# Seven products instead of eight for the last eight pairs of output tiles of the fifth stage, in a decoder step on one core

## The chip, the cores and the metric

The kernel runs on one core of one Trainium2 chip. The metric is the device time of one execution in microseconds; the figures shown are medians of several executions. TensorE does the matrix products, VectorE (DVE) and ScalarE (ACT) work elementwise, GpSimd (POOL) fills buffers and issues some of the DMAs, SyncE (SP) issues the others.

## The reference

1024 prompt tokens and 8 decode tokens, 2048 wide, in fp32, pass through two layers: a pooling layer A, then shared keys and values, then an attention layer B. Cut to what matters here:

```python
# layer A
z = x @ w_in_a                      # 2048 -> 4096: branch u and gate
d = einsum(pool(u) - u, w_grp_a) * scale_a
h = layer_norm(ALPHA * x + (d * silu(gate)) @ w_out_a)
# shared keys and values, 4 heads of 64
kv = h @ w_kv                       # k gets a partial rotary
# layer B: 32 query heads, window of 128, one learned sink per head
z = h @ w_in_b                      # 2048 -> 4096: q and gate
q = rope_partial(z[:, :2048])
o = softmax(q k^T / 8, masked, with sink) @ v
y = layer_norm(ALPHA * h + (o * silu(gate)) @ w_out_b)
```

## The kernel before

**Precision.** A product of fp32 matrices is made on TensorE as three matmuls. Each operand is split into a high part (a cast on ScalarE, L423 for weights, L686 for inputs) and a low part (a subtract on VectorE, L438 and L695). TensorE then forms high x high, high x low and low x high.

**Stages.** Tokens come in two chunks: chunk 0 has 512, chunk 1 has 520 (with the decode tokens). The stages stand in `PHASES`: `ai` (input product of A, with pooling), `ao` (output product of A), `bi` (keys, values, queries and gates, with the attention inside), `bo` (output product of B), each for chunk 0 and then chunk 1. `ai` of chunk 0 is listed as two parts, so `bi` of chunk 0, called the fifth stage here, is the sixth entry of `PHASES`; the sixth stage is `bi` of chunk 1.

**Two ways to multiply.** A stage in `PLAIN` uses `unit`: one output tile of 128 rows is 48 matmuls of 512 columns (L614 to L616). All others use `seven`: the two output tiles of a pair, the even and odd halves of the inner dimension and the two halves of the tokens form a 2 x 2 x 2 block product, which is done with seven products instead of eight (Strassen's way, in Winograd's form). One product is 24 matmuls of 256 or 260 columns (L586 to L588), so a pair takes 168 matmuls of half width where two units take 96 of full width. `ORDER7` and `ORDERL` are orders of the seven products. In exchange `seven` needs sums of weight blocks and sums of input blocks. Before the change `bi` of chunk 0 is plain.

**Weight sums.** A plain stage loads the four blocks of a pair, and `plain_pair` forms the four sums afterwards (L254) and stores them to DRAM; the later chunk loads them in `next_pair`. `first_pair` is for a first chunk that already uses seven products: it forms the sums (L307) ahead of their use and stores them too. For the output weights of B, `sum_gen("wob")` is a side generator: 32 parts, each two loads of 256 KB, three adds (L397 to L399) and a store; half of the parts run in the fifth stage and half in the sixth.

**Input sums.** The sums of the inputs (T1 to T4) are made by `t_ops` (four adds, L741 to L744, and a store), called by `t_gen` (a generator that loads the activations again), by `ln_gen` (the layer norm) or, for the attention's output o, by `gate`. They lie in `Td`.

**Order.** All weight blocks form one `stream`. `begin` runs ahead of TensorE by a fixed number of blocks: load, cast, subtract (7, 4, 3 in stages with seven products, 5, 4, 3 in plain ones). `end` counts steps, runs events due at that step and, every so many steps (`every`), one step of a side generator, if enough of the 53 buffers are free (`room`). Inputs of the next stage are prepared by `x_begin`, `x_tick` and `x_get`: X blocks are loaded (L676), cast and subtracted some steps ahead; at the latest they are made when first asked for. The program order of TensorE, VectorE and ScalarE is the order of the source (`in_order`). Loads are issued on SP's queue, stores of sums on POOL's.

**Attention.** `attend` strings out one tile's work over steps: score (L1456), selection and largest value (L1473 to L1485), exponentials, totals, norm, transposes (`turn`, L1509), copies (L1518, L1519), values (L1533) and the gate (L1542, then a store of o). `q_done` applies the rotary (L1321), which needs a copy of the query with partitions swapped: four DMAs on SP's queue (L1313), then the sum (L1428).

Where a stage of chunk 1 follows one of chunk 0 that also used seven products, three dummy matmuls (L574, `fresh`) stand at its start.

Of the kernel before, what the change touches and what calls it, by code (L numbers as in the profile page):

```python
# [50 lines left out]
    ("ai", 0, (0, 1)), ("ai", 0, (1, 4)), ("ai", 1, (0, 4)), ("ao", 0, None), ("ao", 1, None), ("bi", 0, None),  # L51
    ("bi", 1, None), ("bo", 0, None), ("bo", 1, None),
# [107 lines left out]
class Kern:  # L160
# [132 lines left out]
    def first_pair(self, name, q):  # L293

        a11, a12, a21, a22 = self.quads(name, q)
        ws = self.ws[name][q]
        s = {}

        def load(k, src):
            return self.load1(s, k, src)  # L300

        def add(out, x, y, i):
            def go():
                assert self.prepped >= self.made - 2
                if out not in s:
                    s[out] = self.mem.full()
                self.nc.vector.tensor_add(s[out].a[:, :1024], s[x].a[:, :1024], s[y].a[:, :1024])  # L307
# [26 lines left out]
    def build_stream(self):  # L334
        io = self.io
        w = []
        for kind, c, part in PHASES:
# [4 lines left out]
            if kind == "ai":  # L342
                for g in range(*part):
                    for q in (2 * g, 2 * g + 1, 8 + 2 * g, 9 + 2 * g):
                        w += pr("wia", q)
                    for h in range(2):
                        w.append(self.lone(io["wg"][g][:, h * 1024 : (h + 1) * 1024]))
            elif kind == "bi":
                w += self.next_pairs("wkv", range(2), locked) if seven else pr("wkv", 0) + pr("wkv", 1)
                for p in range(8):  # L350
                    if seven:
                        w += pr("wib", p) + pr("wib", 8 + p)
                    else:
# [14 lines left out]
    def sum_gen(self, name):  # L368
# [15 lines left out]
        for n, (q, cs) in enumerate(parts):  # L384
            one = self.ph == "bi1"
            while one and n not in held and len(self.mem.whole()) < 6 and self.hurry is not name:
                yield
            load(n)
            if not one:
                load(n + 1)  # L390
            yield
            if one:
                yield
            s = held.pop(n)
            t = s.v(4, W)
            add = self.nc.vector.tensor_add
            add(t[:, 0:2, :], t[:, 0:2, :], t[:, 1:3, :])  # L397
            add(t[:, 2, :], t[:, 2, :], t[:, 0, :])
            add(t[:, 3, :], t[:, 3, :], t[:, 2, :])  # L399
            self.nc.gpsimd.dma_start(self.ws[name][q][:, :, cs], t)  # L400
            s.free(True)
            if n % 4 == 3:
                self.summed[name] = q + 1
            yield
# [392 lines left out]
    def ln_gen(self, c, pre, acc, gc, bc, out, td):  # L797
# [29 lines left out]
        else:  # L827
            sq, sqs = self.mem.full(), {}
            for p in range(10):
# [4 lines left out]
                if 1 <= p <= 8:  # L834
                    sqs[p - 1] = sq if p == 1 else self.mem.full()
                    nc.scalar.activation(flat(sqs[p - 1]), flat(pre[p - 1]), AF.Square)
                if p > 2:
# [24 lines left out]
        for p in range(10):  # L862
# [6 lines left out]
            if 1 <= p <= 8:  # L869
                affine(p - 1)  # L870
                if td is None:
                    pre[p - 1].free(True)
            if p >= 2 and td is not None:
# [568 lines left out]
    def attend(self, c, t, at, s1, s2, late=False):  # L1442
# [96 lines left out]
        def gate():  # L1539
            a = self.ao[c, t] = self.mem.half()  # L1540
# [5 lines left out]
            if c == 1 or ("o", c) not in self.Td:  # L1546
                self.ao.pop((c, t)).free(True)
            elif t % 2:
                e = self.ao.pop((c, t - 1))
                self.t_ops(e.a[:, :TP], a.a[:, :TP], self.Td["o", c], t // 2, T // 2)  # L1550
                e.free(True)
                self.ao.pop((c, t)).free(True)
# [139 lines left out]
    def phase_bi(self, c, nxt):  # L1692
        nc = self.nc
        T = CHUNKS[c][1]
        self.kv_open(c)
        if not self.strassen:
# [12 lines left out]
            for t in range(16):  # L1709
# [14 lines left out]
                self.last = t == 15  # L1724
# [3 lines left out]
        pairs = []  # L1728
        for done in (self.k_done, self.v_done):
            box, z0, z1 = self.two(T)  # L1730
            pairs.append((z0, z1, lambda done=done, box=box: done(c, box["s"])))
        self.both(c, *pairs)
        for p in range(8):
# [6 lines left out]
            box, z0, z1 = self.two(T)  # L1740
            if p == 7:
                self.x_begin(nxt)
                self.ahead = 6, 3, 2
            self.pair(c, z0, z1, lambda t0=t0, box=box: self.q_done(c, t0, box["s"], 2, 3))
            self.last = p == 7

            def g_done(t0=t0, box=None, p=p):
                self.gate_done(c, t0, box["s"], 2)
# [3 lines left out]
            box, z0, z1 = self.two(T)  # L1752
            self.pair(c, z0, z1, lambda g=g_done, box=box: g(box=box))
# [30 lines left out]
    def run(self):  # L1784
# [3 lines left out]
        self.sg, self.qs, self.ao = {}, {}, {}  # L1788
# [10 lines left out]
        for n, (kind, c, part) in enumerate(PHASES):  # L1799
# [6 lines left out]
            if n == 0 or (kind, c) == ("bi", 0):  # L1806
# [24 lines left out]
            elif (kind, c) == ("ao", 1):  # L1831
                gen = self.ln_gen(0, *acc[0], C_GA, C_BA, self.act["h", 0], self.Td.get(("h", 0)))
                self.at(3, lambda gen=gen: add(("h", 0, True), gen))
                self.every = 2
            elif (kind, c) == ("bi", 0):
                add(("h", 1, False), self.ln_gen(1, *acc[1], C_GA, C_BA, self.act["h", 1], self.Td.get(("h", 1))))
                self.summed["wob"] = 0
                add("wob", self.sum_gen("wob"))
                self.every = 2
            elif (kind, c) == ("bi", 1):  # L1840
                self.every, self.room = 1, 99
                self.at(14, lambda: setattr(self, "room", 0))
# [11 lines left out]
            elif kind == "bi":  # L1854
                self.phase_bi(c, nxt)
# [148 lines left out]
```

## Time and profile before

| | |
|---|---|
| median of 3 executions | 2384.65 us (2382.46 to 2386.11) |
| the profiled execution | 2384.47 us, its span 2382.7 us |
| mean granted TensorE clock | 0.996 |
| TensorE busy | 2341.7 us, 98% |
| VectorE busy | 1875.5 us, 79% |
| ScalarE busy | 1305.6 us, 55% |
| DMA | 653.25 MB, mean 274 GB/s |

In a row of a group stand the line, the engine, the operation, output <- input, the shapes, the count, then the busy time and the mean of one in ns, then the idle time of the engine just before and what ended it. In a row of a timeline stand the start, the duration, and in brackets the idle time before and its releaser. Matmuls are pipelined, so the duration of one (281 ns) is longer than the distance to the next. In the profile the stages begin at these times of the span: `ai` of chunk 0 at 8.0 (its seven-product part at 111.4), `ai` of chunk 1 at 384.2, `ao` at 755.5 and 916, the fifth stage at 1081.7, the sixth at about 1554, `bo` at 2025 and 2183.4.

### The profile page before, as it was taken

What the parts mean: (1) busy time and instruction counts of PE and PEld (TensorE: products, weight loads), DVE (VectorE), ACT (ScalarE), POOL (GpSimd) and SP (SyncE); (2) the same over time, 40 slices, a digit from 0 to 9 for tenths busy, and PEclk for the clock granted to TensorE, in tenths of its full rate; (3) what the DMA queues carried; (4) which work ended last, traced back from release to release, by engine and by line L of the source; (5) the groups of instructions that cost most, each with busy time, mean ns of one, the idle gap of its engine ahead of it and who ended that gap; (6) DMA issues with size and microseconds to landing.
All of it is one profiled execution on the core that took longest, in us unless ns stands there. A gap on an engine that the chain in (4) does not pass through costs nothing. (4 is left out here: it accounts for less than half of the span.)

```text
span 2382.7 us, 45063 instructions
## 1 busy us (share of the span) xinstructions
PE 2341.7 (98%) x17823; PEld 2198.5 (92%) x17823; DVE 1875.5 (79%) x2327; ACT 1305.6 (55%) x2363; POOL 192.3 (8%) x361
## 2 busy tenths in 40 slices
PE   8999999999999999999999999999999999999996
PEld 6899999999999999998778888899999999999996
DVE  8797999776788768868787777778777667789877
ACT  4454446454446447653564444475666667546655
POOL 0111110000000000000011111101000000000000
PEclk9999999999999999999999999999999999999998
DMA  8767779998889988988587777589786558799884
GB/s 292 243 220 277 257 255 379 310 307 299 299 297 352 313 276 313 353 294 285 186 322 261 263 269 247 202 285 303 254 244 208 173 177 296 226 337 364 303 281 141
DMA packets 250563, 653.25 MB, mean 274 GB/s; under 512 B 25456, under 2 KB 109168, under 8 KB 250352
## 3 DMA queue, kind: packets, MB, share of 16 engines
q1 hardware_dynamic: 206032, 489.50, 61.9%
q0 software_dynamic: 44320, 160.88, 17.5%
q8 instruction: 139, 2.28, 0.4%
q14 instruction: 72, 0.59, 0.1%
HBM read 459.41 MB, written 181.36 MB: 269 GB/s over the span
## 5 line engine op out<-in xcount | busy, mean ns | idle before, releaser
L586 PE MATMUL pD<-m,m 128*128 128x260 f32 (+1 forms) x4304 | 1220.8, 284 | 5.4 <-DVE m L547 3.4
L588 PE MATMUL pD<-m,m 128*128 128x260 f32 (+1 forms) x4304 | 1213.0, 282 | 2.7 <-DVE m L438 2.7
L587 PE MATMUL pD<-m,m 128*128 128x260 f32 (+1 forms) x4304 | 1213.8, 282 | 0.0
L438 DVE TENSOR_TENSOR m<-m,m 128x1024 fp32r<-128x1024 f32 x650 | 785.5, 1219 | 102.4 <-ACT m L423 69.9
L586 PEld LDWEIGHTS pD<-m,m 128*128 128x128 f32 x4304 | 810.8, 188 | 14.2 <-issue 7.6
L588 PEld LDWEIGHTS pD<-m,m 128*128 128x128 f32 x4304 | 811.3, 188 | 3.7 <-DVE m L438 3.5
L587 PEld LDWEIGHTS pD<-m,m 128*128 128x128 f32 x4304 | 810.8, 188 | 1.6 <-issue 1.4
L423 ACT CAST m<-m 128x1024 fp32r<-128x1024 f32 x650 | 676.2, 1048 | 242.8 <-DVE m L307 55.5
L614 PE MATMUL pD<-m,m 128*128 128x512 f32 x704 | 281.6, 400 | 8.0 <-ACT m L686 8.0
L615 PE MATMUL pD<-m,m 128*128 128x512 f32 x704 | 278.4, 395 | 0.8 <-DVE m L695 0.8
L616 PE MATMUL pD<-m,m 128*128 128x512 f32 x704 | 278.1, 395 | 0.0
L614 PEld LDWEIGHTS pD<-m,m 128*128 128x128 f32 x704 | 133.1, 189 | 42.7 <-ACT m L686 8.0
L615 PEld LDWEIGHTS pD<-m,m 128*128 128x128 f32 x704 | 133.2, 189 | 31.4 <-DVE m L695 1.9
L616 PEld LDWEIGHTS pD<-m,m 128*128 128x128 f32 x704 | 133.0, 189 | 30.6
L695 DVE TENSOR_TENSOR m<-m,m 128x1024 fp32r<-128x1024 f32 (+1 forms) x114 | 139.4, 1226 | 10.0 <-ACT m L686 4.3
L686 ACT CAST m<-m 128x1024 fp32r<-128x1024 f32 (+1 forms) x114 | 119.6, 1053 | 19.2 <-PE pD L616 6.2
L559 ACT COPY m<-pD 128x260 f32<-128x260 f32 (+1 forms) x75 | 28.0, 373 | 184.8 <-PE pD L588 184.4
L254 DVE TENSOR_TENSOR m<-m,m 128x1024 f32<-128x1024 f32 x88 | 107.5, 1222 | 1.9
L1492 ACT ACTIVATE m<-m,sm 128x128 f32<-128x128 f32 x256 | 99.3, 390 | 0.0
L547 DVE TENSOR_TENSOR m<-pD,m 128x260 f32<-128x260 f32 (+1 forms) x78 | 33.1, 424 | 80.7 <-PE pD L588 80.6
L954 PE MATMUL pD<-m,m 128*128 128x260 f32 (+1 forms) x528 | 91.3, 323 | 0.0
L552 DVE TENSOR_TENSOR m<-pD,m 128x260 f32<-128x260 f32 (+1 forms) x76 | 32.2, 424 | 71.1 <-PE pD L588 71.1
(197 smaller groups left out, 2136.2 us busy)
## 6 DMA issues: line engine op xcount, KB each, us to landing
m<-in_wia SPq DMA_DIRECT2D x112, 512.0 KB, 7.1
m<-in_wib SPq DMA_DIRECT2D x112, 512.0 KB, 4.9
swia<-m POOLq DMA_DIRECT2D x64, 512.0 KB, 4.8
m<-swia SPq DMA_DIRECT2D x64, 512.0 KB, 7.0
m<-swoa SPq DMA_DIRECT2D x64, 512.0 KB, 6.9
swib<-m POOLq DMA_DIRECT2D x64, 512.0 KB, 5.0
m<-swib SPq DMA_DIRECT2D x64, 512.0 KB, 5.1
m<-swob SPq DMA_DIRECT2D x64, 512.0 KB, 6.5
```

The lines of the kernel that those rows point to most:

```text
L254: self.nc.vector.tensor_add(s[out].a[:, :1024], s[a].a[:, :1024], s[b].a[:, :1024])
L423: self.nc.scalar.copy(hi.r[:, :1024], self.stream[self.cast].src().a[:, :1024])
L438: self.nc.vector.tensor_sub(lo.r[:, :1024], s.src().a[:, :1024], hi.a[:, :1024])
L586: nc.tensor.matmul(ps[:, :TH], wh[:, s], h, start=new and k == 0, stop=False, skip_group_check=on)
L587: nc.tensor.matmul(ps[:, :TH], wh[:, s], l, start=False, stop=False, skip_group_check=on)
L588: nc.tensor.matmul(ps[:, :TH], wl[:, s], h, start=False, stop=k == 7, skip_group_check=on)
L614: nc.tensor.matmul(ps[:], wh[:, s], h, start=par == 0 and k == 0, stop=False)
L615: nc.tensor.matmul(ps[:], wh[:, s], l, start=False, stop=False)
L616: nc.tensor.matmul(ps[:], wl[:, s], h, start=False, stop=par == 1 and k == 7)
L686: self.nc.scalar.copy(h.r[:, :n], s.a[:, :n])
L695: self.nc.vector.tensor_sub(l.r[:, :n], s.a[:, :n], h.a[:, :n])
L1492: nc.scalar.activation(x["s3"][:, i, :], x["s3"][:, i, :], AF.Exp, bias=nm[:, i : i + 1], scale=0.125, accum_out=rs[:, i : i + 1],)
```

## The change

The fifth stage is cut in two entries of `PHASES`. Keys, values and the first four pairs of query tiles and of gate tiles stay plain. The last four pairs of query tiles and four pairs of gate tiles use `seven`. For that the X blocks of the second half are loaded, cast and subtracted anew in the form that `seven` reads, and the sums of h of chunk 0 are made by a `t_gen` in the first half (load, four adds, store, for eight parts).

The weights of these eight pairs now go through `first_pair`: seven blocks per pair are cast and subtracted instead of four, and the four sums come ahead of their use. `first_pair` itself changes: the block a22 is no longer kept from product 2 to product 6 but is added in place and loaded a second time. This holds for the first stage too.

The sums of the output weights (`sum_gen`) run wholly in the sixth stage, with other rules for when a part is loaded and when it is added. The input sums over o of chunk 0 are no longer made in `gate` but by a `t_gen` in the sixth stage. `ln_gen` pauses more often, and the side generators of the first half step every 1.2 steps instead of every 2. The sixth stage now follows one with seven products, so it gets the dummy matmuls of `fresh`. Counted over the whole program the change adds 579 matmuls (768 of 512 columns go, 1344 of 256 columns and three dummies come), 70 instructions on VectorE, 58 on ScalarE, 34 DMA issues on SP and 8 on POOL.

```diff
 PHASES = (
-    ("ai", 0, (0, 1)), ("ai", 0, (1, 4)), ("ai", 1, (0, 4)), ("ao", 0, None), ("ao", 1, None), ("bi", 0, None),
-    ("bi", 1, None), ("bo", 0, None), ("bo", 1, None),
+    ("ai", 0, (0, 1)), ("ai", 0, (1, 4)), ("ai", 1, (0, 4)), ("ao", 0, None), ("ao", 1, None), ("bi", 0, (0, 4)),
+    ("bi", 0, (4, 8)), ("bi", 1, (0, 8)), ("bo", 0, None), ("bo", 1, None),
 )
...
             0: ent("a", [load("a", a11)], [], []),
-            2: ent("e", [load("b", a21), load("c", a22)], [add("e", "b", "c", 1)], []),
+            2: ent("e", [load("b", a21), load("e", a22)], [add("e", "b", "e", 1)], []),
...
-            6: ent("c", [], [], free("c")),
+            6: ent("c", [load("c", a22)], [], free("c")),
...
-        for n, (q, cs) in enumerate(parts):
-            one = self.ph == "bi1"
-            while one and n not in held and len(self.mem.whole()) < 6 and self.hurry is not name:
-                yield
-            load(n)
-            if not one:
-                load(n + 1)
-            yield
-            if one:
-                yield
-            s = held.pop(n)
+        def add(n):
+            q, cs = parts[n]
+            s = held[n]
...
+        if self.ph == "bi1":
+
+            since, n = {}, 0
+            while n < len(parts):
+                hurry = self.hurry is name
+                if n in held and (hurry or self.i - since[n] >= 3):
+                    yield from add(n)
+                    n += 1
+                m = n + len(held)
+                if m < len(parts) and (len(held) < 2 and len(self.mem.whole()) > 5 + len(held) or hurry and not held):
+                    load(m)
+                    since[m] = self.i
+                yield
+            return
...
                     nc.scalar.activation(flat(sqs[p - 1]), flat(pre[p - 1]), AF.Square)
+                yield
...
+            if td is not None:
+                yield
             if p >= 2 and td is not None:
...
         def gate():
-            a = self.ao[c, t] = self.mem.half()
+            a = self.mem.half()
...
-            elif t % 2:
-                e = self.ao.pop((c, t - 1))
-                self.t_ops(e.a[:, :TP], a.a[:, :TP], self.Td["o", c], t // 2, T // 2)
...
-            for t in range(16):
+            for t in range(2 * ps[0], 2 * ps[-1] + 2):
...
-                self.attend(c, t, 8, {13: 13, 15: 11}.get(t, 14), 2, t > 13)
+                self.attend(c, t, 8, 14 if t <= 2 * ps[-1] else 9, 2)
                 self.unit(q_done)
-                if t == 12:
+                if t == 2 * ps[-1] + 0:
                     self.x_begin(nxt)
...
-            if n == 0 or (kind, c) == ("bi", 0):
+            if n == 0 or (kind, c) == ("bi", 0) and self.wide:
...
-                gen = self.ln_gen(0, *acc[0], C_GA, C_BA, self.act["h", 0], self.Td.get(("h", 0)))
+                gen = self.ln_gen(0, *acc[0], C_GA, C_BA, self.act["h", 0], None)
...
-            elif (kind, c) == ("bi", 0):
+            elif (kind, c) == ("bi", 0) and not self.strassen:
                 add(("h", 1, False), self.ln_gen(1, *acc[1], C_GA, C_BA, self.act["h", 1], self.Td.get(("h", 1))))
+                add(("h", 0, False), self.t_gen(("h", 0)))
+                self.every = 1.2
+            elif (kind, c) == ("bi", 1):
                 self.summed["wob"] = 0
-                add("wob", self.sum_gen("wob"))
-                self.every = 2
-            elif (kind, c) == ("bi", 1):
-                self.every, self.room = 1, 99
-                self.at(14, lambda: setattr(self, "room", 0))
+                self.at(14, lambda: add("wob", self.sum_gen("wob")))
+                self.at(14, lambda: add(("o", 0, False), self.t_gen(("o", 0))))
+                self.every, self.room = 1, 0
```

More of the change, by code (lines that the diff above doesn't have):

```diff
@@ L348, in build_stream @@
             elif kind == "bi":
[L349 to L351 removed]
+                if part[0] == 0:
+                    w += self.next_pairs("wkv", range(2), locked) if seven else pr("wkv", 0) + pr("wkv", 1)
+                if seven:
+                    for p in range(*part):
                         w += pr("wib", p) + pr("wib", 8 + p)
[L353 removed]
+                else:
+                    for p in range(*part):
                         q, g = pr("wib", p), pr("wib", 8 + p)
@@ L403, in sum_gen @@
                 self.summed[name] = q + 1
+        if self.ph == "bi1":
[11 more added lines that the diff above has]
+            return
+        for n in range(len(parts)):
+            load(n)
+            load(n + 1)
+            yield
+            yield from add(n)
             yield
@@ L1727, in phase_bi, with queries @@
             return
[L1728 to L1733, printed above, removed]
+        if ps[0] == 0:
+            pairs = []
+            for done in (self.k_done, self.v_done):
+                box, z0, z1 = self.two(T)
+                pairs.append((z0, z1, lambda done=done, box=box: done(c, box["s"])))
+            self.both(c, *pairs)
+        def queries(p):
             t0 = 2 * p
@@ L1854, in run @@
             elif kind == "bi":
-                self.phase_bi(c, nxt)
+                self.phase_bi(c, range(*part), nxt)
             else:
```

36 lines of the change are left out of this document (21 added, 15 removed).

## The prediction

> **What bounds the kernel now.** I read the page's engine totals first, then its costliest groups, then the busy time of each engine by stage, then TensorE's timeline.
>
> ```profile
> span 2382.7 us, 45063 instructions
> PE 2341.7 (98%) x17823; PEld 2198.5 (92%) x17823; DVE 1875.5 (79%) x2327; ACT 1305.6 (55%) x2363; POOL 192.3 (8%) x361
> ```
> ```profile
> 111.40:125.00 13.60, 13.60 (x117) 13.55 (x116) 13.57 (x13) 8.47 (x12) 1.30 (x4) 1.00 0.79 276
> 111.40:384.20 272.80, 271.56 (x2162) 265.02 (x2161) 244.19 (x291) 137.26 (x196) 32.80 (x71) 1.00 0.75 263
> 384.20:755.50 371.30, 369.42 (x3077) 368.82 (x3076) 289.71 (x435) 180.02 (x284) 30.36 (x48) 1.00 0.91 314
> 1430.00:1554.00 124.00, 124.00 (x684) 100.41 (x681) 90.10 (x115) 63.76 (x163) 17.73 (x34) 1.00 0.67 225
> 1554.00:2025.00 471.00, 469.97 (x4186) 454.56 (x4186) 345.36 (x439) 313.34 (x718) 22.15 (x36) 1.00 0.75 242
> 1722.00:1822.00 100.00, 100.00 (x912) 96.76 (x911) 72.87 (x95) 65.20 (x161) 5.80 (x9) 1.00 0.75 235
> ```
>
> TensorE is busy for 98% of the span. In the last part of the fifth stage (1430 to 1554) and in the middle of the sixth (1722 to 1822) it never stands: there, time is TensorE's work and nothing else. The columns are length, busy time of PE, weight load, DVE, ACT and POOL, granted clock, DMA share and GB/s. So the change gains by what it takes off TensorE, and loses wherever VectorE or a DMA then comes late.
>
> **The gain on TensorE.** Every tile of the fifth and sixth stages begins its attention with the score (L1456).
>
> ```profile
> 1320.00 0.70 PE L1456 MATMUL pS<-m,m 64*128 64x256 f32 x4
> 1536.89 0.70 PE L1456 MATMUL pS<-m,m 64*128 64x256 f32 x4
> 1692.69 0.70 PE L1456 MATMUL pS<-m,m 64*128 64x256 f32 x4
> 1792.83 0.70 PE L1456 MATMUL pS<-m,m 64*128 64x256 f32 x4
> 1552.82 1.03 PE L1509 MATMUL pS<-cst,m 128*128 128x128 f32 x8
> 1559.35 1.97 PE L1533 MATMUL pO<-m,m 128*64 128x128 f32 x32
> 1564.30 2.00 PE L1456 MATMUL pS<-m,m 64*128 64x256 f32 x16
> 889.73 0.28 PE L586 MATMUL pD<-m,m 128*128 128x256 f32 x1
> 893.96 0.28 PE L586 MATMUL pD<-m,m 128*128 128x256 f32 x1
> ```
>
> The first two scores stand 8 plain tiles apart: 216.89 / 8 = 27.11 us. Attention takes 2.00 + 1.03 + 1.97 = 5.0 of it. The other 22.11 are 96 matmuls of 512 columns (two units of 48), 0.2303 each. The next two scores stand 4 tiles of the sixth stage apart: 25.04 each. There the two tiles of a pair share 14 products of 24 matmuls, 168 per tile, 260 columns wide. The change has 256 columns: between the last two rows lie 36 matmuls of that width (12 times L586, L587, L588), 4.23 / 36 = 0.1175 each. A changed tile takes 5.0 + 168 x 0.1175 = 24.74. Over eight tiles, tiles 8 to 15: 8 x 2.37 = **19.0 us gained**. That the sixth stage already runs this form, with the same three PSUM banks and the same attention, covers the bank copies too.
>
> **VectorE inside the eight pairs.** The half gets 24 more weight subtracts and casts (L438, L423) than it had, since 7 blocks per pair replace 4.
>
> ```profile
> L438 DVE TENSOR_TENSOR m<-m,m 128x1024 fp32r<-128x1024 f32 x650 | 785.5, 1219 | 102.4 <-ACT m L423 69.9
> L254 DVE TENSOR_TENSOR m<-m,m 128x1024 f32<-128x1024 f32 x88 | 107.5, 1222 | 1.9
> L307 DVE TENSOR_TENSOR m<-m,m 128x1024 f32<-128x1024 f32 x48 | 58.7, 1222 | 6.2 <-DMA m<-in_wia 5.3
> L397 DVE TENSOR_TENSOR m<-m 128x512 f32<-128x512 f32 x64 | 43.5, 680 | 2.0 <-DMA m<-in_wob 2.0
> L399 DVE TENSOR_TENSOR m<-m 128x256 f32<-128x256 f32 x64 | 27.2, 425 | 2.2
> L741 DVE TENSOR_TENSOR m<-m 128x256 f32<-128x256 f32 x16 | 6.7, 417 | 0.0
> ```
>
> The block sums are four per pair as before, made ahead of their use (L307) instead of after it (L254). Two tiles of the sixth stage cost VectorE 72.87 / 2 = 36.4 us; less its share of the output-weight sums, plus 8 L307 at 1.22 = 9.8. A part of those sums costs 0.680 + 2 x 0.425 = 1.53, and 16 parts over 471 us are 2.6 per two tiles. So 43.6 busy in 49.5: 88%. The nearest stage with seven products and their own sums (111.40 to 384.20) has VectorE at 244.19 of 272.80, 90%, and TensorE lost 1.24 us in all. ScalarE has 65.20 of 100 in the sixth stage and no sums to add. I take 0, cover VectorE's 12% of slack; bounds 0 and, by rival D, +17.
>
> **The entry into the seven-product half.** All 14 half-blocks of X for this half are new: 14 loads, casts (L686) and subtracts (L695), beside the first pair's weights and sums, while tiles 6 and 7 still run their attention. In the order of the changed kernel VectorE has, from tile 6's gate (which must follow its values on TensorE) through the last X subtract of the first pair, 55 instructions: 37 of 1024 columns, 2 predicated copies, 7 of 512 columns, 9 small.
>
> ```profile
> 1224.84 1.22 DVE L438 TENSOR_TENSOR m<-m,m 128x1024 fp32r<-128x1024 f32 x1
> 1225.98 2.48 DVE L254 TENSOR_TENSOR m<-m,m 128x1024 f32<-128x1024 f32 x2
> 1401.44 0.69 DVE L1542 SCALAR_TENSOR_TENSOR m<-pO,m 128x512 f32<-128x512 f32 x1 [2.13 <-PE pO L1533]
> 1406.78 1.31 DVE L1477 COPY_PREDICATED m<-mki,pS 128x1024 f32<-128x1024 int32 x1
> ```
>
> Back to back one follows the other after 1225.98 - 1224.84 = 1.14. So 37 x 1.14 + 2 x 1.31 + 7 x 0.61 (0.69 less the same 0.08) and an estimate of 1.3 for the small ones: 50.4 us. TensorE's work over that stretch is two scores, one turn and one values (7.0), 84 plain matmuls (19.3) and 156 narrow ones (18.3): 44.6. VectorE is **5.8 late**. Bounds: 0, since the only other change from plain to seven (111.40 to 125.00) had VectorE full for 13.57 of 13.60 and TensorE never stood; 9.7, if each instruction cost its whole duration. I take 5.8, nearer to the order's count.
>
> A stall costs more than itself:
>
> ```profile
> 1237.16 2.51 PE L1456 MATMUL pS<-m,m 64*128 64x256 f32 x16 [2.32 <-DVE m L1428]
> ```
> ```profile
> 1234.70:1237.30 2.60, 0.28 (x6) 0.14 (x4) 2.18 (x4) 0.33 (x1) 0.00 (x0) 1.00 1.00 360
> 1237.30:1239.60 2.30, 2.30 (x17) 1.48 (x17) 2.27 (x5) 0.00 (x0) 0.53 (x1) 0.76 0.99 375
> 1239.60:1242.00 2.40, 2.40 (x8) 1.92 (x7) 2.37 (x7) 1.74 (x2) 0.56 (x1) 0.51 0.97 320
> 1242.00:1245.00 3.00, 3.00 (x15) 2.44 (x14) 2.97 (x4) 0.00 (x0) 0.53 (x1) 1.00 1.02 380
> ```
>
> TensorE stood 2.32, and the granted clock then fell to 0.76 and 0.51: 0.24 x 2.3 + 0.49 x 2.4 = 1.7 us more. One such loss, **+2** (0 to 4). The Trainium skill ("TensorE: Matmul & The Clock Gate", "What's actually happening") halves the clock after an idle window of about 3.4 us; with several shorter stalls this term would be 0 and the sum 2374. The 2.32 us row above doesn't agree, so the measurement decides.
>
> **DMA.** Added are 20 weight loads (a22 is read again for product 6; 12 of them at 111 to 384), 14 X loads, 16 loads and 8 stores for the sums over inputs (L741 to L744; those of h are new, in the first half; those of o move from the gate to the sixth stage).
>
> ```profile
> m<-in_wib SPq DMA_DIRECT2D x112, 512.0 KB, 4.9
> m<-h SPq DMA_DIRECT2D x16, 512.0 KB, 6.9
> swib<-m POOLq DMA_DIRECT2D x64, 512.0 KB, 5.0
> m<-m SPq DMA_DIRECT2D x64, 64.0 KB, 4.2
> ```
> ```profile
> 1235.09 1.29 DVE L1321 TENSOR_TENSOR m<-m,m 128x512 f32<-128x512 f32 x2 [2.05 <-DMA m<-m]
> ```
>
> The 12 add 6.3 MB to 272.8 us, 263 to 286 GB/s; the next stage moves 314 and TensorE loses 1.88 of 371: price 0. In the three plain tiles (81.3 us) before the first new X is used, the changed order has 14 weight loads, 16 sum stores, 8 h loads, 8 stores of their sums and 14 X loads of 0.52 MB, with swaps and o 33.0 MB: 406 GB/s. SP's queue carries loads and the rotary swaps (m<-m) in one line; what stands behind a late swap is all of VectorE, as at 1235.09. Much of it may be spread earlier, so I take 0; bounds -4 (the stall at 1237 disappears, since the sums of the output weights leave that stage) to +10 (rival C).
>
> **The rest.** The sixth stage now starts after a seven-product stage and gets the three dummy matmuls that other such starts have (L574):
>
> ```profile
> 2184.46 0.39 PE L574 MATMUL pD<-m,m 128*128 128x260 f32 x1 [0.61 <-ACT m L559]
> ```
>
> 0.61 + 3 x 0.12 = **+1.0** (0.4 to 1.1). It also takes the other 16 parts of the output-weight sums (24.5 us of VectorE) and 32 sums over o (L741's 0.42 each): 345.36 + 38 = 383 of 471, 81%, still under the 90% shown harmless; for its entry, where they meet new X blocks, **+2** (0 to 5). The layer-norm generator's extra yields move work within the first half at no cost that a row shows: 0, or a stall of 1237's size, 4.
>
> **Sum.** The profiled execution is 2384.47 (1.77 outside its span), 0.18 under the median. 2384.5 - 19.0 + 5.8 + 2 + 1 + 2 = **2376**.
>
> **Rivals.** A is this forecast, 2371 to 2380. B: the entry is covered as at 111.40 and the 1237 stall goes; 2384.5 - 19.0 + 1 + 2 = 2368, less 4 = 2364; taken as 2366. For it: 111.40 to 125.00. Against: at 111 four X blocks are made on the chip and no attention runs. C: the burst of 33.0 MB can't go in 81.3 us. At the 380 GB/s of 1242 it takes 86.8, at the 360 of 1234.70 it takes 91.7: 5.5 to 10.4 late, so 2382 to 2387, say 2384, no change. For it: DMA share 1.00 at 360. Against: a third of the bytes are stores that nobody waits for soon. The Trainium skill ("DMA: Bandwidth & Descriptors", "Where 436 GB/s comes from") says that HBM transfers are bound at about 358 GB/s and not by the fabric's 435; by the first C comes true at its upper end, by the second the burst fits and C falls. The 375 and 380 above pass 358 for some 5 us, so neither is confirmed over 81. D, slower: in each of the 56 products the subtract of the next block comes late, because VectorE is in order and waits in attention (L1542 stood 2.13 for its values); 0.3 us each is 17, 2393. It decides against no change from 8.3 / 56 = 0.15 each. For it: 88% busy with waits that the stage at 111 doesn't have. Against: 1722 to 1822 has those waits and TensorE is full.
>
> **How the numbers follow.** A 0.40, B 0.15, C 0.22, D 0.23. Under 0.2% (4.8 us) a measurement of this kernel can't be told from no change. Faster is B and nearly all of A, 0.54; same C and A's edge, 0.23; slower D, 0.23. The range leaves out D's upper half and B's tail: 2363 to 2393; A's own is 2371 to 2380.
>
> **What would show it.** Scores in the new half 49.5 us per two tiles (right) or over 52 (D). TensorE idle before the first narrow products ended by VectorE's X subtract: 4 to 8 us with a clock under 1 behind it (A), none (B), or ended by DMA m<-h, m<-th or m<-m with a share of 1.00 (C). TensorE idle in the sixth stage above 5 us would make it wrong elsewhere.

## The result and the profile after

The changed kernel takes 2419.51 us (2415.43 to 2420.71), the one before, run beside it, 2385.38 us. The ratio is 1.0142, with an interval of 1.0124 to 1.0159: it is **34 us slower**, where 2376 with a range to 2393 was predicted. The profiled execution took 2415.43 us, the fastest of the four.

From the page of the changed kernel:

```profile
span 2413.7 us, 46600 instructions
PE 2335.0 (97%) x18402; PEld 2222.6 (92%) x18402; DVE 1929.3 (80%) x2397; ACT 1344.6 (56%) x2421; POOL 196.2 (8%) x369
...
L605 PE MATMUL pD<-m,m 128*128 128x260 f32 (+1 forms) x4752 | 1343.3, 283 | 23.7 <-DVE m L455 23.7
L603 PE MATMUL pD<-m,m 128*128 128x260 f32 (+1 forms) x4752 | 1350.0, 284 | 6.8 <-DVE m L564 3.4
L604 PE MATMUL pD<-m,m 128*128 128x260 f32 (+1 forms) x4752 | 1341.7, 282 | 6.5 <-DVE m L712 6.5
...
L307 DVE TENSOR_TENSOR m<-m,m 128x1024 f32<-128x1024 f32 x80 | 97.8, 1222 | 17.9 <-DMA m<-in_wib 7.2
```

The kernel before had, for the first of these matmuls:

```profile
L588 PE MATMUL pD<-m,m 128*128 128x260 f32 (+1 forms) x4304 | 1213.0, 282 | 2.7 <-DVE m L438 2.7
```

TensorE's busy time fell by 6.7 us and the span grew by 31.0. Before, the matmuls of the weight stream waited 2.7 us for the weight subtract (then L438); now (L455) it is 23.7. New beside it are 6.5 us for the X subtract (L712).

Where the time went can be read from the scores of the tiles' attention, which both kernels run. These are the changed kernel's, from the timeline of TensorE:

```profile
1291.50 1.78 PE L1476 MATMUL pS<-m,m 64*128 64x256 f32 x14
1426.72 1.57 PE L1476 MATMUL pS<-m,m 64*128 64x256 f32 x12
1525.92 1.35 PE L1476 MATMUL pS<-m,m 64*128 64x256 f32 x10
1648.96 2.00 PE L1476 MATMUL pS<-m,m 64*128 64x256 f32 x16
2053.61 1.57 PE L1476 MATMUL pS<-m,m 64*128 64x256 f32 x12
```

The kernel before has the same tiles here:

```profile
1292.91 1.35 PE L1456 MATMUL pS<-m,m 64*128 64x256 f32 x10
1645.41 1.35 PE L1456 MATMUL pS<-m,m 64*128 64x256 f32 x10
2023.41 1.35 PE L1456 MATMUL pS<-m,m 64*128 64x256 f32 x10
```

Tiles 9 and 13 of the fifth stage, the second and third row after, are 4 tiles apart: 99.20 / 4 = 24.80 each. That is the 24.74 of the prediction. The other rows (tile 5, the first and the last tile of the sixth stage) cut the time into pieces:

| piece | after against before |
|---|---|
| start to tile 5's score | -1.4 |
| tile 5 to the sixth stage's first score | +5.0, where -19.0 was the gain: **23.9 lost** |
| first to last score of the sixth stage | **+26.7** |
| rest | +0.8 |

In the first piece the first stage ends 2.4 late, and the stall that stood at 1237 is gone. I call the second piece the *entry loss* (difference plus the gain, 18.96 unrounded) and the third the *sixth stage's loss*.

TensorE's stops around the new half, from its timeline; the first seven sum to 14.7 us, and the last comes when the half is left:

```profile
1319.79 2.00 PE L1476 MATMUL pS<-m,m 64*128 64x256 f32 x16 [1.11 <-DVE m L1448]
1351.77 0.70 PE L1553 MATMUL pO<-m,m 128*64 128x128 f32 x4 [6.43 <-ACT m L1538]
1353.07 3.25 PE L1553 MATMUL pO<-m,m 128*64 128x128 f32 x28 [0.60 <-DVE m L1539]
1369.52 0.39 PE L604 MATMUL pD<-m,m 128*128 128x256 f32 x1 [0.62 <-DVE m L712]
1371.79 0.38 PE L604 MATMUL pD<-m,m 128*128 128x256 f32 x1 [0.58 <-DVE m L712]
1375.20 0.39 PE L604 MATMUL pD<-m,m 128*128 128x256 f32 x1 [1.73 <-DVE m L712]
1380.47 0.39 PE L604 MATMUL pD<-m,m 128*128 128x256 f32 x1 [3.59 <-DVE m L712]
1539.12 0.39 PE L605 MATMUL pD<-m,m 128*128 128x256 f32 x1 [2.23 <-DVE m L455]
```

VectorE, in the same stretch, begins with the gate behind tile 6's score (it is tile 4's gate: a gate stands two tiles behind its score) and waits once, for a weight block:

```profile
1323.18 0.68 DVE L1562 SCALAR_TENSOR_TENSOR m<-pO,m 128x512 f32<-128x512 f32 x1
...
1333.73 1.23 DVE L307 TENSOR_TENSOR m<-m,m 128x1024 f32<-128x1024 f32 x1 [7.00 <-DMA m<-in_wib]
...
1379.23 2.32 DVE L712 TENSOR_TENSOR m<-m,m 128x1024 fp32r<-128x1024 f32 x2
```

From 1323.18 to the end of the last X subtract at 1381.55 are 58.4 us: the 50.4 that were counted, plus the 7.0 of this wait, within 1.0. Less the 44.6 of TensorE's work that the prediction set against them, they make TensorE 13.8 late; its six stops from 1351.77 to 1380.47 sum to 13.6. The X subtract (L712) ends four of these, 6.5 in all. The two at the values (L1553) are 7.0. By the rows the longer one comes by way of ScalarE, which stood until VectorE, behind the late block, had prepared the exponentials (L1505), and was then late with the copy (L1538) that the values need:

```profile
1339.02 0.21 ACT L1510 ACTIVATE sm<-sm 128x8 f32<-128x8 f32 x1 [14.48 <-DVE sm L1505]
```

The late block was issued late, as SyncE's queue shows:

```profile
1319.01 0.45 SPq L248 DMA_DIRECT2D m<-in_wib  x1
1325.96 1.54 SPq L693 DMA_DIRECT2D m<-h  x2
1327.60 5.64 SPq L248 DMA_DIRECT2D m<-in_wib  x2
```

Weight loads (L248) stand in line behind X loads (L693), and for 6.5 us nothing was issued. Three rows of the waits of that queue from 1265 to 1385 (releaser, total, count, longest) say for what; the 6.5 is in the first:

```profile
SPq L693 <- DMA swib<-m: 12.8, 3, 6.5
SPq L248 <- DVE m L712: 11.2, 1, 11.2
SPq L693 <- DMA th<-m: 7.1, 2, 6.7
```

The loads wait for buffers: until a store out of one has landed, or VectorE has read it. Other rows name TensorE as the reader, and the rotary swaps (L1333).

In the sixth stage the two largest stops, and what VectorE waited for ahead of each:

```profile
1877.45 0.58 PE L605 MATMUL pD<-m,m 128*128 128x260 f32 x1 [8.80 <-DVE m L455]
1971.90 0.59 PE L605 MATMUL pD<-m,m 128*128 128x260 f32 x1 [4.50 <-DVE m L455]
```
```profile
1876.17 1.23 DVE L455 TENSOR_TENSOR m<-m,m 128x1024 fp32r<-128x1024 f32 x1 [10.15 <-DMA o<-m]
...
1969.15 0.43 DVE L758 TENSOR_TENSOR m<-m 128x256 f32<-128x256 f32 x1 [4.64 <-DMA m<-o]
```

The first is a weight subtract that waits for a *store* of o: what lies in its destination buffer is not stored yet. The second stands behind the reloading of o for its sums.

### The profile page after: what moved, and what is told of

The parts are those of the page before. It is cut to its first block, busy times and chain, and to the rows that moved or that the text cites. A ratio compares the mean times of both kernels' runs of the same rounds, so it can differ in the third digit from the quotient of the medians.

```text
span 2413.7 us, 46600 instructions
## 1 busy us (share of the span) xinstructions
PE 2335.0 (97%) x18402; PEld 2222.6 (92%) x18402; DVE 1929.3 (80%) x2397; ACT 1344.6 (56%) x2421; POOL 196.2 (8%) x369
## 5 line engine op out<-in xcount | busy, mean ns | idle before, releaser
L605 PE MATMUL pD<-m,m 128*128 128x260 f32 (+1 forms) x4752 | 1343.3, 283 | 23.7 <-DVE m L455 23.7
L603 PE MATMUL pD<-m,m 128*128 128x260 f32 (+1 forms) x4752 | 1350.0, 284 | 6.8 <-DVE m L564 3.4
L604 PE MATMUL pD<-m,m 128*128 128x260 f32 (+1 forms) x4752 | 1341.7, 282 | 6.5 <-DVE m L712 6.5
L605 PEld LDWEIGHTS pD<-m,m 128*128 128x128 f32 x4752 | 897.7, 189 | 27.3 <-DVE m L455 26.9
L603 PEld LDWEIGHTS pD<-m,m 128*128 128x128 f32 x4752 | 897.3, 189 | 18.3 <-issue 10.1
L604 PEld LDWEIGHTS pD<-m,m 128*128 128x128 f32 x4752 | 897.2, 189 | 9.0 <-DVE m L712 7.3
L455 DVE TENSOR_TENSOR m<-m,m 128x1024 fp32r<-128x1024 f32 x674 | 814.6, 1219 | 102.6 <-ACT m L440 60.4
L440 ACT CAST m<-m 128x1024 fp32r<-128x1024 f32 x674 | 701.3, 1047 | 273.5 <-DVE m L307 60.3
L631 PE MATMUL pD<-m,m 128*128 128x512 f32 x448 | 178.9, 399 | 8.2 <-ACT m L703 8.2
L632 PE MATMUL pD<-m,m 128*128 128x512 f32 x448 | 176.9, 395 | 1.2 <-DVE m L712 1.2
L633 PE MATMUL pD<-m,m 128*128 128x512 f32 x448 | 176.8, 395 | 0.0
L712 DVE TENSOR_TENSOR m<-m,m 128x1024 fp32r<-128x1024 f32 (+1 forms) x128 | 156.3, 1225 | 9.6 <-PE pD L632 4.1
L703 ACT CAST m<-m 128x1024 fp32r<-128x1024 f32 (+1 forms) x128 | 133.7, 1050 | 11.8 <-PE pD L633 6.2
L307 DVE TENSOR_TENSOR m<-m,m 128x1024 f32<-128x1024 f32 x80 | 97.8, 1222 | 17.9 <-DMA m<-in_wib 7.2
L631 PEld LDWEIGHTS pD<-m,m 128*128 128x128 f32 x448 | 84.6, 189 | 29.5 <-ACT m L703 8.4
L632 PEld LDWEIGHTS pD<-m,m 128*128 128x128 f32 x448 | 84.6, 189 | 21.0 <-DVE m L712 2.2
L633 PEld LDWEIGHTS pD<-m,m 128*128 128x128 f32 x448 | 84.5, 189 | 19.5
L564 DVE TENSOR_TENSOR m<-pD,m 128x260 f32<-128x260 f32 (+1 forms) x86 | 36.4, 424 | 76.0 <-PE pD L605 75.7
L974 PE MATMUL pD<-m,m 128*128 128x260 f32 (+1 forms) x528 | 91.3, 323 | 0.0
L569 DVE TENSOR_TENSOR m<-pD,m 128x260 f32<-128x260 f32 (+1 forms) x84 | 35.6, 424 | 65.4 <-PE pD L605 65.4
```

Of the source, the lines that this page charges most:

```text
L440: self.nc.scalar.copy(hi.r[:, :1024], self.stream[self.cast].src().a[:, :1024])
L455: self.nc.vector.tensor_sub(lo.r[:, :1024], s.src().a[:, :1024], hi.a[:, :1024])
L603: nc.tensor.matmul(ps[:, :TH], wh[:, s], h, start=new and k == 0, stop=False, skip_group_check=on)
L604: nc.tensor.matmul(ps[:, :TH], wh[:, s], l, start=False, stop=False, skip_group_check=on)
L605: nc.tensor.matmul(ps[:, :TH], wl[:, s], h, start=False, stop=k == 7, skip_group_check=on)
L631: nc.tensor.matmul(ps[:], wh[:, s], h, start=par == 0 and k == 0, stop=False)
```

## The experiments

All edits are made on the changed kernel. "First stage" is how late the dummies at the end of `ai` of chunk 0 stand. Losses are those defined above, from the same scores in each trace (us); the ratio is to the kernel before. e4 and e10 leave sums out and e8 the dummies: these three are read for their times alone.

| run | ratio (interval) | first stage | entry | sixth stage |
|---|---|---|---|---|
| the change | 1.0142 (1.0124 to 1.0159) | 2.4 | 23.9 | 26.7 |
| e1 h sums from layer norm | 1.0142 (1.0127 to 1.0157) | 1.8 | 22.1 | 30.2 |
| e2 buffer freed late | 1.0101 (1.0086 to 1.0117) | 3.2 | 26.5 | 15.6 |
| e3 o sums in the gate | 1.0082 (1.0065 to 1.0099) | 3.2 | 24.6 | 16.7 |
| e4 entry without sums | 1.0116 (1.0099 to 1.0133) | 3.2 | 18.9 | 26.6 |
| e5 = e2 + e3 | 1.0041 (1.0026 to 1.0056) | 1.6 | 23.7 | 6.1 |
| e6 X blocks earlier | 1.0049 (1.0033 to 1.0066) | 3.5 | 16.2 | 16.3 |
| e7 X loads on GpSimd's queue | 1.0163 (1.0143 to 1.0183) | 1.7 | 39.1 | 24.3 |
| e8 a22 kept, no dummies | 1.0115 (1.0099 to 1.0130) | 0.0 | 27.9 | 23.0 |
| e9 mends together | 1.0047 (1.0034 to 1.0060) | 0.3 | 21.0 | 8.8 |
| e10 = e9 without entry sums | 1.0015 (1.0003 to 1.0027) | 0.1 | 11.6 | 7.9 |
| e11 = e9, 8 sums on GpSimd | 1.0057 (1.0043 to 1.0070) | 0.0 | 21.6 | 8.2 |
| e12 = e9, shorter lookahead | 1.0043 (1.0028 to 1.0058) | 0.6 | 17.4 | 6.9 |
| e13 = e5, lookahead 6, 4, 3 | 1.0039 (1.0026 to 1.0051) | 1.7 | 22.9 | 1.7 |
| e14 = e12 + that lookahead | 1.0035 (1.0022 to 1.0047) | 0.2 | 16.1 | 2.9 |

Entries and sixth stages that an edit doesn't touch scatter by 2 to 4 us, so differences below that are not read.

**e1, the sums of h from the layer norm.**

```diff
-gen = self.ln_gen(0, *acc[0], C_GA, C_BA, self.act["h", 0], None)
+gen = self.ln_gen(0, *acc[0], C_GA, C_BA, self.act["h", 0], self.Td["h", 0])
...
-add(("h", 0, False), self.t_gen(("h", 0)))
```

> The sums over h of chunk 0 are made by the layer norm in the second output stage of layer A, from data still on the chip, instead of being made in the fifth stage after loading h again: 8 loads and 8 stores of 0.5 MB and 32 adds leave the three plain tiles ahead of the entry. Theory DMA (the entry loses 23 us because the queue of SyncE stands behind buffers whose stores are still in the air, so that a weight block arrives 7.0 us late and all of VectorE behind it): from tile 6's score to the first score of the sixth stage 329 us become 318 or less, the wait of L307 for m<-in_wib falls under 2, the total falls by 10 to 18. Theory count (VectorE simply has too many instructions between tile 6's gate and the first pair's last X subtract): these instructions stay, so the total stays within 5 of the changed kernel.

The entry loses 22.1, and the total stays, as the theory of the count had it. The share of the DMAs (next to last number) ahead of the entry fell to 0.45 and 0.66, where the changed kernel has 1.00 and 0.95; the windows of e1 from 1290 on:

```profile
1290.00:1310.00 20.00, 20.00 (x118) 16.06 (x117) 10.58 (x14) 9.22 (x27) 0.73 (x2) 1.00 0.45 132
1310.00:1330.00 20.00, 20.00 (x123) 16.19 (x122) 10.84 (x12) 7.88 (x12) 2.82 (x6) 1.00 0.66 224
```

and yet VectorE waited for the same block, 7.76 us:

```profile
1334.12 1.23 DVE L307 TENSOR_TENSOR m<-m,m 128x1024 f32<-128x1024 f32 x1 [7.76 <-DMA m<-in_wib]
```

So the burst of bytes (rival C) was there and is not the cause of this wait. The block is late because it is issued late, here too behind X loads, one of which waited 5.3 us for a store of o out of its buffer (SyncE's queue in e1, then its waits from 1318 to 1334):

```profile
1329.50 0.46 SPq L248 DMA_DIRECT2D m<-in_wib  x1
```
```profile
SPq L693 <- DMA o<-m: 5.3, 1, 5.3
```

That is the other half of the theory of DMA, and e1 doesn't test it: the waits for buffers stayed.

**e2, the decode step's buffer.**

```diff
             x["v"].free(True)
-            W.free()
+            W.free(True)
```

> The buffer W of the decode step is marked as stored when it is given back, so that it is not the next one to be taken. Theory buffer: the subtract that waited 10.15 for o<-m at 1866 waits for this buffer alone, whose 32 KB store was issued behind four loads of the output-weight sums; the stop of TensorE of 8.8 at 1877 goes, total 9 to 12 lower. Theory load: the sixth stage is short of DMA time because all 32 parts of the sums are in it, and the stop only moves to another instruction: total within 4.

No stop of TensorE is left between 1855 and 1905, and the sixth stage loses 11.1 less. The buffer's 32 KB store was issued at 1870.01, behind four loads of the output-weight sums that took the queue from 1865.65:

```profile
1865.65 3.63 SPq L384 DMA_DIRECT2D m<-in_wob  x4
1869.37 0.55 SPq L248 DMA_DIRECT2D m<-swib  x1
1870.01 0.38 SPq L1694 DMA_DIRECT2D o<-m  x1
```

The wait was for this one buffer, as the first theory had it.

**e3, the sums of o.** The generator for ("o", 0) in the sixth stage goes, and `gate` gets its lines of before back.

> The sums over o of chunk 0 go back into the gate of the fifth stage (as before the change), and the generator that loads o again in the sixth stage is left out. Theory: the loss at tile 11 and 12 of the sixth stage (8 us; L758 waits 4.64 for m<-o) goes, total 7 to 10 lower, and the entry of the seven-product half grows by 0 to 4 for 4 more adds per pair of tiles. Rival: the output-weight sums fill the place and the stage still loses over 20, total within 4.

The sixth stage loses 10.0 less, a little more than expected; the entry is within the scatter. The total fell by 14 by the ratios, more than the 7 to 10 expected, but by 8.1 between the profiled executions, from which the losses are read.

**e4, the entry without sums.**

```diff
-self.nc.vector.tensor_add(...)      # add1 of query and gate pair 3, first_pair of pair 4
 self.nc.gpsimd.dma_start(...)
```

> Leaves out the adds (not the stores) of the weight sums of the last plain query and gate pair and of the first two pairs with seven products: 16 adds of 1.22 us less on VectorE around the entry, same DMAs; what is stored there are single blocks, not sums. Theory count: 11 to 16 of these lie in the 55 instructions, 12.5 us and more are taken from VectorE, and the lateness of the entry goes nearly whole: total 12 to 20 lower. Theory DMA: VectorE, or ScalarE ahead of it, waits for the same late weight block, total 3 to 8 lower only.

The total fell by about 6, as the theory of the late block had it (3 to 8) and not the count (12 to 20). As it said, ScalarE now waited for in_wib (21.7 us in four waits from 1290 to 1420, against 3.5 in the changed kernel). The entry loses 18.9, 5 better. This trace has stops of 5.2 us of its own at tile 6's score, ahead of the half; from 1345 to 1420 TensorE stands 4.7 us, against 13.6 in the changed kernel. The adds of the first pair, left out here, are those that waited for the late block, so the run takes away the count and that wait together.

**e5, e2 and e3 together.**

> The edits of the second and the third experiment together. Theory: their causes are separate (one buffer; the burst of sums over o), so the loss within the sixth stage, 26.7 us in the changed kernel and 15.6 and 16.7 with one of them, falls under 8, and the total to 2393 to 2398. Rival: the sixth stage is short of time for all 32 sum parts, and a new wait takes the place: loss over 12, total over 2401.

The sixth stage's loss falls to 6.1, under the 8 expected: the two causes are separate and add up.

**e6, X blocks earlier.** With e1 and e2, and

```diff
-                if t == 2 * ps[-1] + 0:
+                if t == 2 * ps[-1] - 1:
...
-        spare = 3 if self.last else X_KEEP + {"bi0": 4, "bi1": 2, "bo0": 1}.get(self.ph, 0)
+        spare = 3 if self.last else X_KEEP + {"bi0": 2, "bi1": 2, "bo0": 1}.get(self.ph, 0)
```

> Sums over h from the layer norm (first experiment), decode buffer freed late (second), and the new X blocks for the half with seven products begun one tile earlier and with 7 free buffers asked for instead of 9: 7 of the 14 X subtracts stand ahead of the first narrow product instead of 5. Theory lead: the entry (22.1 us lost in the first experiment) falls to 10 to 17. Theory buffers: the X blocks take the buffers that the weights need, loads on the queue of SyncE wait longer, and the entry stays at 20 or more.

16.2 against the 22.1 of e1, as the theory of lead says. Whether a longer lead gains more was not run.

**e7, X loads on the other queue.**

```diff
-        self.nc.sync.dma_start(t, src)
+        q = self.nc.gpsimd if <fifth stage, X of ("h", 0)> else self.nc.sync
+        q.dma_start(t, src)
```

> The 14 loads of the new X blocks are issued on GpSimd's queue instead of SyncE's, so that weight loads don't stand behind an X load that waits for its buffer; decode buffer freed late as in the second experiment. Theory queue: the wait of L307 for m<-in_wib (7.0) falls under 2 and the entry from 24 to 26 lost to 17 or less. Rival, buffers: the weight load has to wait for a buffer of its own, and the entry stays at 21 or more.

Worse: 39.1. The wait of L307 for in_wib fell from 7.00 to 4.38, not under 2, and VectorE now waits for stores of sums, whose queue the X loads share:

```profile
1365.23 1.23 DVE L455 TENSOR_TENSOR m<-m,m 128x1024 fp32r<-128x1024 f32 x1 [10.42 <-DMA swib<-m]
```

This fits the rival: a load that waits for a buffer holds up what stands behind it, on either queue. It is read from the waits; no run had more buffers.

**e8, a22 kept.** The two lines of `first_pair` as before the change, and `self.fresh` not set for `bi`.

> The block a22 is kept from product 2 to product 6 as before the change (20 loads of 0.5 MB fewer, one buffer more held), and the three dummy matmuls at the start of the sixth stage are left out. Theory load: the 2.4 us that the changed kernel is late at the end of the first stage fall under 0.7, and the entry gets 1 to 4 better. Theory buffer: the first stage stays 1.8 or more late, or the entry gets 2 or more worse. Without the dummies the sixth stage starts 0.4 to 1.1 earlier.

The first stage is no longer late: 0.0 here and 0.0 to 0.6 in the five later runs that keep a22 in that stage alone (e9 to e12, e14), against 1.6 to 3.5 in all that load it twice. The entry gets 4.0 worse, as the theory of buffers has it, at the edge of the scatter. What the dummies cost can't be told from the scatter here.

**e9, all mends.** e1, e2, e3, a22 kept in the first stage alone, and e6 asking for 6 free buffers instead of its 7 (the edit has 6, not the 5 of the text below).

> Sums over h from the layer norm, sums over o in the gate, decode buffer freed late, a22 kept in the first stage only, new X blocks begun one tile earlier with 5 free buffers asked for: 7 of 14 X subtracts stand ahead of the first narrow product. If the causes add up: first stage late by under 0.7 instead of 2.4; entry loses 13 to 17 instead of 24; sixth stage 7 to 9 instead of 27; total 2381 to 2388, the same as the kernel before. If a new wait takes their place: over 2392.

A miss: 2396.2 us. First stage and sixth stage came as expected; the entry lost 21.0 instead of 13 to 17. It has e3's adds over o on VectorE, which e6 hadn't, but that these take the difference wasn't tried.

**e10, the same without sums at the entry.**

> The ninth experiment, and the adds of the weight sums of the last plain pairs and of the first two pairs with seven products left out (stores kept; single blocks are stored instead of sums). Theory count (with the X blocks earlier, what is left of the entry is VectorE's number of instructions): 10 to 14 adds of 1.14 go from the entry, its loss falls from 13 to 17 to under 6. Theory buffers: late loads and late X blocks keep it at 10 or more.

The entry loses 11.6, 9.4 less than in e9: short of the count's "under 6", and by the letter on the side of the buffers. The windows from 1345 to 1420, PE busy first: the changed kernel, e9, and e10:

```profile
1345.00:1420.00 75.00, 61.44 (x523) 58.04 (x523) 66.64 (x71) 48.60 (x99) 8.66 (x17) 0.93 0.72 237
```
```profile
1345.00:1420.00 75.00, 68.70 (x592) 65.05 (x592) 67.00 (x78) 48.84 (x103) 8.97 (x18) 0.95 0.73 253
```
```profile
1345.00:1420.00 75.00, 75.00 (x657) 71.39 (x656) 63.22 (x74) 50.83 (x106) 8.92 (x18) 1.00 0.72 244
```

In e10 TensorE never stands there. Two things keep this from showing that the count alone held it. In e9 the first of the sums left out still waits for its weight block (first row), and that wait goes with the sum. And e10 had a stop ahead of tile 5's score (second row), outside the piece, which gave VectorE a lead:

```profile
1328.80 1.23 DVE L307 TENSOR_TENSOR m<-m,m 128x1024 f32<-128x1024 f32 x1 [5.21 <-DMA m<-in_wib]
```
```profile
1298.11 2.50 PE L1480 MATMUL pS<-m,m 64*128 64x256 f32 x10 [3.98 <-DVE m L1452]
```

From tile 4's score to the sixth stage's first, which takes in that stop, e10 is 5.9 shorter than e9; by the medians it is 6.4 (2389.78 against 2396.2). So VectorE's sums at the entry, their work and their wait together, hold TensorE there, and how the two share it stays open. The 11.6 that the piece still loses lie outside this window: 2.4 between the scores of tiles 5 and 6, at a clock lowered by a stop just ahead of them, and the rest behind the half's last tiles, with a stop of 3.33 where the half is left and a granted clock of 0.92 and 0.74 in the 20 us around it. The stop at the leaving is in every trace with this half (2.23 in the changed kernel); its cause was not tried.

**e11, the last plain sums on GpSimd.**

> The ninth experiment, and the 8 adds of the last plain query and gate pair are done by GpSimd, whose sums nobody needs for 400 us. Theory count: 8 times 1.14, 9.1 us, go from VectorE, the entry loses 5 to 10, total 3 to 9 under the ninth experiment and under the kernel before. Theory buffers: an add on GpSimd takes longer than 1.14 and holds its four blocks longer, so buffers come later: entry as in the ninth or worse.

No better (2399.63). Two rows of e11, VectorE and GpSimd:

```profile
1323.73 3.89 DVE L458 TENSOR_TENSOR m<-m,m 128x1024 fp32r<-128x1024 f32 x1
```
```profile
1324.14 2.40 POOL L255 TENSOR_TENSOR m<-m,m 128x1024 f32<-128x1024 f32 x1
```

While GpSimd adds for 2.40 us, the subtract on VectorE takes 3.89 instead of 1.22. Beside the eight adds VectorE's instructions take about 10 us longer in all (a sum from the trace), against the 9.1 that the move takes off it: it frees nothing.

**e12, shorter lookahead at the entry.**

> The ninth experiment, with weights taken 6, 3 and 2 blocks ahead instead of 7, 4 and 3 during the first pair with seven products: two to three buffers fewer are held by weights, and the weight subtracts stand one block later. Theory buffers: entry 2 to 5 better than in the ninth. Theory count: the same instructions stand in the same stretch, within 2.

Entry 17.4 against 21.0 (and 16.1 in e14, which has the same edit): in favour of buffers, at the edge of the scatter, and the total (2396.53) is no different from e9.

**e13, lookahead in the sixth stage.** On e5:

```diff
                 self.every, self.room = 1, 0
+                self.at(14, lambda: setattr(self, "ahead", (6, 4, 3)))
```

> The fifth experiment (decode buffer freed late, sums over o in the gate), and from step 14 of the sixth stage on weights are loaded, cast and subtracted 6, 4 and 3 blocks ahead instead of 6, 3 and 2; before the change it was 7, 4 and 3. Theory lookahead: with two blocks ahead the subtract stands right behind a copy (L569) that waits for TensorE, so TensorE then waits for it; with three it is a product earlier, and the stage loses under 3 us instead of 7.9: total 4 to 7 under the fifth experiment. Theory load: the same adds of the moved sums stay on VectorE, and the stage still loses over 6.

The sixth stage's loss falls from 6.1 to 1.7, as expected of the lookahead, but the total doesn't fall by 4 to 7: the medians differ by 2.2, and the ratios, 1.0039 and 1.0041, hardly. Between the last score and the dummies of `bo` this run is 3.8 later than the kernel before, e5 only 1.5, so about half of the gain is lost again there; why was not tried. The changed code sets `self.ahead = 6, 3, 2` at the last pair of any half with seven products, now also at the end of the fifth stage, and nothing resets it until `bo`.

**e14, everything together.**

> The twelfth experiment (all mends, shorter lookahead at the entry) with the lookahead of the thirteenth. If the causes found add up: first stage under 0.7 late, entry 13 to 16 lost of the 19 gained, sixth stage under 3 lost: total 2382 to 2388, the same as the kernel before. If something else holds the time: over 2392.

2392.55 us, 27 us better than the change and, at 1.0035, still slower than the kernel before, above the expected 2382 to 2388. Against e12 the sixth stage's loss falls from 6.9 to 2.9, and the stretch from its last score to the dummies of `bo` goes from 1.9 late to 5.8: nearly all of it is lost again. No version beat the kernel before.

## Why the prediction was wrong

- **Gain of 19.0: right.** 24.80 us per tile against 24.74, and VectorE 83.69 busy of 100 in the middle of the half with TensorE at 99.93 (1400 to 1500). Rival D fell: its 0.3 us per product would make a tile 2.1 longer.
- **Entry, 5.8 + 2: the step that failed first.** The count was right (50.4 of VectorE's work, found again within 1.0; the gate where it starts is tile 4's, and its upper bound comes to 9.3, not 9.7), and so was A's sign, stops of 6.5 us that end with the X subtract. But VectorE was taken to run without a wait. It waited 7.0 us for a weight block behind X loads without a buffer, which added to the 5.8 and, by the rows, reached TensorE at the values by way of ScalarE. The bound at zero, from the change at 111.40, was the wrong neighbour: no attention runs there, and most of the new X comes from data on the chip. At the new entry 16 buffers of the old X and 28 of the new meet in 53. Stops of 14.7 and a slower clock took the place of 5.8. That the load was late for want of a buffer is read from the queue's waits; of the 16 to 22 us that e9, e11, e12 and e14 still lose here, the shares of the count, the wait and the leaving stay open.
- **Clock, +2 (0 to 4): too small.** At the entry the granted clock was 0.50 from about 1351 to 1357 and from 1381 to 1384.5, about 4 us more by windows of 1 us; one stop in the sixth stage cost another 2.7 (last section).
- **DMA at the entry, 0: wrong, and not by rival C.** The DMAs were as full as that rival said (380 GB/s from 1280 to 1300), but the wait was for in_wib, and e1 shows that bytes weren't its cause. That loads *queue for buffers*, not for bandwidth, was in none of the cases.
- **First stage, 0 for 12 more loads of a22: mis-sized**, 2.4; e8 gives 0.0 with the old lines.
- **Stall at 1237, bound -4: it went.** From tile 2's score to tile 4's it took 58.2 us before and 54.2 after, 4.0 less.
- **Sixth stage, +2 (0 to 5): the other step that failed**, with 26.7. It was costed as VectorE's load alone (81%), which was right as a load (378.55 us busy of the 497 from 1560 on, against the 383 forecast) and priced none of three things: a buffer handed to its next user while its store still stood in the queue (11.1 by e2), sums over o that come in a burst behind their own loads (10.0 by e3), and a setting of the lookahead that the shared code now leaves on (4.4 by e13, 4.0 by e14 against e12). The first two show in the total; of the third most is lost again behind the last score.

## What to carry to other kernels

- An engine's count of instructions gives how late it is only if it never waits; when a stage change needs two sets of operands at once, count free buffers step by step first, since a load without a buffer holds up everything behind it on its queue.
- A share of busy time (81%, 88%) says nothing of a stage whose waits are for single buffers: look up who frees a buffer, when its store is *issued*, and who takes it next.
- When code for one stage is shared with another, follow every setting it leaves behind.

## What the runs showed of the hardware

Behind a long stop TensorE's granted clock fell to half. After the stop of 8.80 that ended at 1877.45, in the changed kernel's windows (granted clock third from the end):

```profile
1878.00:1880.00 2.00, 2.00 (x11) 2.00 (x10) 2.00 (x2) 0.00 (x0) 0.00 (x0) 0.50 0.79 186
1880.00:1882.00 2.00, 2.00 (x11) 2.00 (x11) 1.05 (x3) 0.00 (x0) 0.50 (x1) 0.50 0.19 76
1882.00:1884.00 2.00, 2.00 (x15) 2.00 (x15) 1.30 (x2) 1.38 (x3) 0.21 (x1) 0.79 0.64 209
1884.00:1886.00 2.00, 2.00 (x19) 2.00 (x18) 1.91 (x3) 0.39 (x3) 0.00 (x0) 1.00 0.81 236
```

That is about 2.7 us more (0.50 of the 4.55 from 1877.45, 0.21 of 2). The Trainium skill ("TensorE: Matmul & The Clock Gate", "What's actually happening") gives two states, full and half, which these rows agree with.

Shorter stops of one length differ. After the 2.24 us that ended at 1534.53 in e4 the clock stayed full for 1.3 us and was then half until about 1539.2; after the 2.23 us that ended at 1539.12 in the changed kernel it stayed full (1.00 in every window of 1 us to 1545).

DMAs ran at 380 GB/s over 20 us (1280 to 1300 of the changed kernel):

```profile
1280.00:1300.00 20.00, 20.00 (x122) 16.15 (x122) 16.33 (x30) 7.79 (x20) 2.99 (x6) 1.00 1.02 380
```

This is above the 358 that the Trainium skill ("DMA: Bandwidth & Descriptors", "Where 436 GB/s comes from") takes as the bound for transfers with HBM, so that bound doesn't hold for this core here; its 435 for the fabric is not passed.

Beside an add on GpSimd, whose operands lie in SBUF, VectorE's instructions with two operands in SBUF took longer: in e11 3.89 for 1.22, 2.77 for 0.69 and 2.55 for 1.22, beside adds of 2.40. Those that read one operand only (L1504, 1.22) or one from PSUM (L1542, 1.22) took their usual time beside such an add.
